# Modulation weights in steps of one k tile, and raw weight buffers in three smaller pieces

## The chip, the cores and the metric

One core of a Trainium2 chip runs the whole program in one launch. TensorE (PE) multiplies matrices, VectorE (DVE) and ScalarE (ACT) work on tiles in SBUF and PSUM, GpSimd (POOL) on tiles in SBUF, and SyncE (SP) issues every transfer from and to device memory. Each engine works through its own queue in order and waits at semaphores for the others. The metric is the device time of one execution in microseconds.

## The reference

Two layers of a transformer trunk, for 128 context tokens and 512 latent tokens (640 rows in all, width 1024):

```python
mod_ctx = (silu(c_ctx) @ w_mod[l] + b_mod[l])     # 1024 -> 6 * 1024
mod_lat = (silu(c) @ w_mod[l] + b_mod[l])
sh1, sc1, g1, sh2, sc2, g2 = split(mod, 6)
h = rmsnorm(x, norm1) * (1 + sc1) + sh1
proj = h @ w_in + b_in             # queries, keys, values, gates of three mixers
...                                # mLSTM, differential attention, neighbourhood attention
merged = gate0 * (o_da @ w_up_da) + gate1 * (o_ml @ w_up_ml) + gate2 * (o_na @ w_up_na)
x = x + g1 * (merged @ w_out)
h2 = rmsnorm(x, norm2) * (1 + sc2) + sh2
x = x + g2 * (square(relu(h2 @ w_ff1 + b_ff1)) @ w_ff2 + b_ff2)
```

The modulation is a product of two vectors (c and c_ctx) with a 1024 x 6144 matrix for each layer. It depends on no activation, so it can be worked out at any time before its values are used.

## The kernel before

**The large products.** All weights are fp32 and are split into a high part (a cast to fp32r on ACT, `whi`) and a low part (a subtraction on DVE, `wlo`), in `split`. A product is three matmuls: high by high, high by low, low by high. Weights come in blocks of 1 MB (512 KB for the `w_up` matrices) into one of two `raw` buffers of 128 x 2048 (`w_raw`, `NRAW = 2`), and the split writes them into four pairs of `whi`/`wlo` tiles (`NWT = 4`), two pairs to a block. In a-mode (weights stationary) a block is split by columns into two halves, in b-mode (weights streamed) by k tiles.

**The order of the work.** In `layer_mixers` three calls of `drive` run 12, 12 and 20 units. A unit is one block's worth of projection: it yields after each PSUM bank (4 times in a-mode, 5 in b-mode, 2 in an up unit), and after its first yield the next unit's weights are asked for. Between the yields `drive` advances the stages of the three mixers at a rate (`R_ML`, `R_DA`, `R_NA`). `layer_ff` then runs a list of 33 items through `sequence`: the product with `w_out` and the residual (`residual_pass`), the two MLP matrices in turn (`ff1`, `ff2`), and a last residual pass that also prepares the next layer.

**The modulation in the background.** The first 4 of layer 0's 12 chunks (512 columns each) are made at the start by PE. The other 8 of layer 0 and all 12 of layer 1 are made on DVE by a generator (`bg`, with `mod_chunk_dve`): for each k tile two instructions multiply 128 x 512 weights by the two vectors' scalars and add to two accumulators `macc` (of which there are two buffers in all); after 8 k tiles PE transposes the accumulators in 8 pieces, DVE sums along rows and `mod_store` adds the bias. After a layer's last chunk `mod_rows` writes the gates to device memory (`gd`), from where `layer_ff` reads them back as rows (`gload`, tiles `gr`). The weights of a chunk come as two loads of 1 MB into the same `raw` buffers that the projections use. `background()` runs the generator to its next yield. In layer 0's mixers it is called after every second unit from unit 8 to unit 40 (`BG_UNITS`), 17 times, which is just what 8 chunks of 2 steps and `mod_rows` need. In layer 0's MLP it is called at the places of `FF1_BG` and `FF2_BG`, 53 times, where 51 are needed. `layer_ff` starts with `while l not in self.gd: self.background()`.

**Who orders the queues.** The order in which the code names instructions is a priority. The framework's scheduler places each engine's instructions, and one that is ready and has its buffers may stand ahead of one named earlier. Buffers of one tag are handed out in the order in which the code asks for them.

In layer 1 there is no background work in either part, so its stages are the same program without it.

Of the kernel before, what the change touches and what calls it, by code (L numbers as in the profile page):

```python
# [11 lines left out]
F32 = mybir.dt.float32  # L12
F32R = mybir.dt.float32r
AF = mybir.ActivationFunctionType
ALU = mybir.AluOpType
AX = mybir.AxisListType
# [3 lines left out]
P = 128  # L20
D = 1024
KD = D // P
# [64 lines left out]
class Builder:  # L87
    def __init__(self, tc, I, O):
        self.tc, self.nc, self.I, self.O = tc, tc.nc, I, O
        self.uid = 0  # L90
        self.bg = None
        self.units_run = 0
        self.alt = False
        self.ff_phase = False

# [40 lines left out]
    def w_raw(self, src):  # L136

        nk, c = src.shape[1], src.shape[2]
        raw = self.T(self.wp, [P, 2048], F32, "raw", NRAW)
        r3 = raw[:, :nk * c].rearrange("p (k c) -> p k c", k=nk)  # L140
        self.nc.sync.dma_start(r3, src)
        return r3

    def w_tiles(self, n, nk):

# [3 lines left out]

        return self.w_amode_split(self.w_raw(src))  # L150

    def w_amode_split(self, r3):
        nk = r3.shape[1]
        out = []
        for j in range(2):
            h, lo = self.w_tiles(nk * P, nk)
            self.split(h, lo, r3[:, :, j * P:(j + 1) * P])
            out.append((h, lo))
        return out

    def w_bmode(self, src, extra=None):

        r3 = self.w_raw(src)
        rx = None
        if extra is not None:
            rx = self.T(self.wp, [P, 8, 16], F32, "rx", 1)
            self.nc.sync.dma_start(rx, extra)
        return self.w_bmode_split(r3, rx)

    def w_bmode_split(self, r3, rx=None):  # L170
        nk, nco = r3.shape[1] // 2, r3.shape[2]
        w = nco if rx is None else nco + 16
        out = []
        for j in range(2):
            h, lo = self.w_tiles(nk * w, nk)
            ks = slice(j * nk, (j + 1) * nk)
            self.split(h[:, :, :nco], lo[:, :, :nco], r3[:, ks, :])
            if rx is not None:
                self.split(h[:, :, nco:], lo[:, :, nco:], rx[:, ks, :])
            out += [(h[:, k, :], lo[:, k, :]) for k in range(nk)]  # L180
        return out

# [122 lines left out]
            self.modc[l][:, :, 4 * n:4 * n + 4], src,  # L305
            cv2[:, 4 * n:4 * n + 4].unsqueeze(1).to_broadcast([P, 2, 4]), op=ALU.add)

    def mod_chunk_dve(self, l, n):

        nc, I = self.nc, self.I  # L310
        acc = [self.T(self.wp, [P, 512], F32, "macc", 2) for _ in range(2)]
        for kh in range(2):
            raw = self.T(self.wp, [P, 2048], F32, "raw", NRAW)
            r3 = raw.rearrange("p (k c) -> p k c", k=4)
            nc.sync.dma_start(r3, I["w_mod"][l, n, kh])
            for k in range(4):
                kk = kh * 4 + k
                for v in range(2):
                    s = self.cc3[:, v, kk:kk + 1]
                    if kk == 0:  # L320
                        nc.vector.tensor_scalar_mul(acc[v], r3[:, k, :], s)
                    else:
                        nc.vector.scalar_tensor_tensor(acc[v], r3[:, k, :], s, acc[v], op0=ALU.mult, op1=ALU.add)  # L323
                if kk in ((1, 3, 5) if l else (3,)):
                    yield
        red = self.st(8)
        for v in range(2):
            tp = self.t_ps()
            for j in range(4):
                nc.tensor.transpose(tp[:, j * P:(j + 1) * P], acc[v][:, j * P:(j + 1) * P], self.ident)  # L330
            nc.vector.tensor_reduce(red[:, 4 * v:4 * v + 4], tp.rearrange("p (j c) -> p j c", j=4), axis=AX.X, op=ALU.add)
        self.mod_store(l, n, red.rearrange("p (v j) -> p v j", v=2))
        yield

    def mod_norm_cols(self, l, which):

# [145 lines left out]
        return g  # L482

    def w_up(self, src):
        r3 = self.w_raw(src)
        h, lo = self.w_tiles(1024, 4)
        self.split(h, lo, r3)
        return [(h[:, :, q * P:(q + 1) * P], lo[:, :, q * P:(q + 1) * P]) for q in range(2)]
# [25 lines left out]
    def drive(self, units, stages, rate, w, tail):  # L514

        units = list(units)
        credit = 0.0
        waiting = None  # L520
        sdone = False

        def step_stage():
            nonlocal waiting, sdone
            while True:
                if sdone:
                    return
# [12 lines left out]
                return  # L540

        def pick():
            for i, u in enumerate(units):
                if u[2] is None or u[2] in self.labels:
                    return units.pop(i)
            return units.pop(0) if units else (tail, None, None)

        cur = units.pop(0)
        while cur[1] is not None:
            while cur[2] is not None and cur[2] not in self.labels:  # L550
                step_stage()
            nxt = pick()
            wn = None
            first = True
            for _ in cur[1](w):
                if first:
                    wn = nxt[0]()
                first = False
                credit += rate
                while credit >= 1.0:  # L560
                    credit -= 1.0
                    step_stage()
            self.units_run += 1
            if self.units_run in BG_UNITS:
                self.background()
            cur, w = nxt, wn
        while not sdone:
            step_stage()
        return w
# [888 lines left out]
    def layer_ff(self, l, merged, w, last):  # L1458
        tc, nc, I, O = self.tc, self.nc, self.I, self.O
        with tc.tile_pool(name=f"xp{l}", bufs=1, reuse_waits="tile") as xp:  # L1460
# [33 lines left out]
            def ff1_first():  # L1494
                def prep():
                    return self.w_amode(I["w_ff1"][l, 0]), self.w_raw(I["w_ff1"][l, 1])

                def run(wr):
                    w = wr[0] + self.w_amode_split(wr[1])
                    us[0] = [(self.act_slice(), self.act_slice()) for _ in range(4)]  # L1500
                    for a, b in BANKS:
                        for j in range(4):
                            o = self.gemm_a(w[j], h2, a, b)
                            self.ff1_evac(l, j, *us[0][j], o, a, b)
                            if a == 0 and todo:
                                todo.pop(0)()
                            yield a > 0 and j >= 1
                    self.background()
                return prep, run

            def ff1(ch, i):
                def run(w):
                    if i == 0:
                        us[ch] = [(self.act_slice(), self.act_slice()) for _ in range(4)]
                    for q in range(2):
                        j = ch * 4 + i + q
                        for a, b in BANKS:
                            o = self.gemm_a(w[q], h2, a, b)
                            self.ff1_evac(l, j, *us[ch][i + q], o, a, b)
                            if (q, a) in FF1_BG:  # L1520
                                self.background()
                            yield True
                    if i == 0 and 1 <= ch <= TT:
                        t = ch - 1
                        nc.gpsimd.tensor_tensor(xs[t], xs[t], gr[4 if t < 4 else 5], op=ALU.add)
                return (lambda: self.w_amode(I["w_ff1"][l, (ch * 4 + i) // 2])), run

            def ff2(ch, cp):
                def run(w2):
                    sl = slice(cp * 512, (cp + 1) * 512)  # L1530
                    for t in range(TT):
# [1 line left out]
                        tmp = self.T(xp, [P, 512], F32, "tmp", 2)  # L1533
                        nc.vector.tensor_tensor(tmp, o, gr[2 if t < 4 else 3][:, sl], op=ALU.mult)  # L1534
                        nc.gpsimd.tensor_tensor(xs[t][:, sl], xs[t][:, sl], tmp, op=ALU.add)  # L1535
                        if t in FF2_BG:
                            self.background()
                        yield True
                return (lambda: self.w_bmode(I["w_ff2"][l, ch, cp])), run

# [125 lines left out]
    def run(self):  # L1666
        tc, nc, I = self.tc, self.nc, self.I
        with ExitStack() as ctx:
# [4 lines left out]
            def bg():  # L1673
                for l in range(DEPTH):
                    if l:
# [3 lines left out]
                        yield  # L1679
                        yield  # L1680
                        fin()
                    for n in range(4 if l == 0 else 0, 12):
                        yield from self.mod_chunk_dve(l, n)
                    self.mod_rows(l)
                    yield
            self.bg = bg()
# [3 lines left out]


NMM, NS2, NTP = 2, 2, 2
NRAW, NWT = 2, 4
FIN_AT, PREP_AT, FIRST = 4, 3, 7
R_ML, R_DA, R_NA = 1.1, 1.6, 1.6
ML_FIRST = 2
CARRY = 3
LAG1, LAG2 = 1, 1
FF1_BG, FF2_BG = ((0, 0), (1, 256)), (1, 3)
BG_UNITS = range(8, 42, 2)  # L1700
NSL, NOT, NV = 16, 12, 9

OUT_SHAPES = {
# [12 lines left out]
def lay_out(x):  # L1716
# [9 lines left out]
    def halves(w):  # L1726
# [16 lines left out]
        "w_up_na": blocks(x["w_up_na"], 256),  # L1743
        "w_out": halves(x["w_out"]),
        "w_ff2": halves(x["w_ff2"]),
        "w_mod": x["w_mod"].reshape(L, 2, 4, P, 12, 512).transpose(0, 4, 1, 3, 2, 5),
        "w_mod0": x["w_mod"][0, :, :2048].reshape(KD, P, 2048),
        "xT": xs.T.reshape(KD, P, NT).transpose(1, 0, 2),
        "x_sample": x["x_sample"],
# [37 lines left out]
```

## Time and profile before

| | |
|---|---|
| median of 3 runs | 2491.02 us (2487.69 to 2491.09) |
| the profiled execution, its own time | 2490.52 us |
| its span, first to last instruction | 2488.7 us |
| PE busy | 2415.0 us, 97% of the span |
| DVE busy | 1523.0 us, 61% |
| ACT busy | 905.1 us, 36% |
| mean granted TensorE clock | 0.993 of full speed |
| transferred | 286.52 MB, 115 GB/s over the span |

The profile is one execution, 1.8 us longer outside its span than inside it. PE's busy time counts overlapping matmuls once; a gap in it is time in which PE waited.

### The profile page before, as it was taken

Reading aid. Unit: us, or ns where it says so; the run is one execution under the profiler, and the core shown is the slowest. Engines: PE = TensorE matmul, PEld = TensorE weight load, DVE = VectorE, ACT = ScalarE, POOL = GpSimd, SP = SyncE. Lnnn points to the kernel's source line nnn. Section 1 sums busy time; section 2 is a strip of 40 time slices with the busy share of each in tenths; the row PEclk is TensorE's granted clock in tenths of the full one; section 3 lists DMA queues with packets and bytes.
Section 4 is the critical chain, followed back from the end, with each engine's and each line's share of the span. In section 5 each row is a group of like instructions: output and inputs, shape, how many; then the busy total and the mean of one; then the engine's idle time right before and its main releaser. Section 6 shows DMA issues by size and latency. Waiting matters only on the chain. (4 is left out here: it accounts for less than half of the span.)

```text
span 2488.7 us, 39544 instructions
## 1 busy us (share of the span) xinstructions
PE 2415.0 (97%) x15776; PEld 2266.3 (91%) x15776; DVE 1523.0 (61%) x2804; ACT 905.1 (36%) x1954; POOL 640.9 (26%) x701
## 2 busy tenths in 40 slices
PE   6999999999999999999999999999999999999998
PEld 4999999999998898999989999999989889999997
DVE  5557788566634899998565547674443464444444
ACT  4332354334433422223353334443443353322232
POOL 0122122233412233332021212222352312233301
PEclk8999999999999999999999999999999999999999
DMA  7323323333353334444332222223232722222221
GB/s 271 105 94 117 112 97 135 121 117 123 139 190 130 119 136 152 153 136 153 103 122 97 96 90 87 76 82 111 74 116 86 261 85 85 68 85 68 85 68 60
DMA packets 73706, 286.52 MB, mean 115 GB/s; under 512 B 9889, under 2 KB 21249, under 8 KB 49969
## 3 DMA queue, kind: packets, MB, share of 16 engines
q1 hardware_dynamic: 73520, 283.99, 33.3%
q8 instruction: 124, 2.03, 0.3%
q14 instruction: 62, 0.50, 0.1%
HBM read 257.60 MB, written 26.35 MB: 114 GB/s over the span
## 5 line engine op out<-in xcount | busy, mean ns | idle before, releaser
L191 PE MATMUL mm<-act,whi 128*128 128x384 f32 (+1 forms) x2176 | 699.4, 321 | 11.7 <-DVE act L503 3.4
L192 PE MATMUL mm<-act,whi 128*128 128x384 f32 (+1 forms) x2176 | 687.5, 316 | 0.0
L193 PE MATMUL mm<-act,wlo 128*128 128x384 f32 (+1 forms) x2176 | 686.0, 315 | 0.0
L217 ACT CAST whi<-raw 128x1024 fp32r<-128x1024 f32 x296 | 310.9, 1050 | 921.3 <-PE mm L192 439.3
L218 DVE TENSOR_TENSOR wlo<-raw,whi 128x1024 fp32r<-128x1024 f32 x296 | 383.8, 1297 | 381.3 <-ACT whi L217 327.2
L191 PEld LDWEIGHTS mm<-act,whi 128*128 128x128 f32 x2176 | 413.9, 190 | 17.5 <-issue 6.0
L192 PEld LDWEIGHTS mm<-act,whi 128*128 128x128 f32 x2176 | 414.3, 190 | 0.0
L193 PEld LDWEIGHTS mm<-act,wlo 128*128 128x128 f32 x2176 | 413.8, 190 | 0.0
L1535 POOL TENSOR_TENSOR x<-x,tmp 128x512 f32<-128x512 f32 x120 | 194.0, 1623 | 448.5 <-DVE tmp L1534 448.5
L210 PE MATMUL mm<-whi,act 128*128 128x256 f32 (+2 forms) x800 | 270.0, 338 | 0.0
L212 PE MATMUL mm<-whi,act 128*128 128x256 f32 (+2 forms) x800 | 267.1, 334 | 0.0
L211 PE MATMUL mm<-wlo,act 128*128 128x256 f32 (+2 forms) x800 | 266.4, 333 | 0.0
L323 DVE SCALAR_TENSOR_TENSOR macc<-raw,cc,macc 128x512 f32<-128x512 f32 x280 | 232.2, 874 | 20.0 <-DMA raw<-w_mod 19.6
L212 PEld LDWEIGHTS mm<-whi,act 128*128 128x128 f32 x800 | 152.0, 190 | 14.3
L211 PEld LDWEIGHTS mm<-wlo,act 128*128 128x128 f32 x800 | 152.1, 190 | 14.0
L210 PEld LDWEIGHTS mm<-whi,act 128*128 128x128 f32 x800 | 152.1, 190 | 14.0
L210 PE MATMUL t<-whi,act 128*128 128x512 f32 (+1 forms) x416 | 158.5, 381 | 1.7 <-ACT act L217 1.5
L211 PE MATMUL t<-wlo,act 128*128 128x512 f32 (+1 forms) x416 | 157.8, 379 | 0.0
L212 PE MATMUL t<-whi,act 128*128 128x512 f32 (+1 forms) x416 | 157.8, 379 | 0.0
L192 PE MATMUL t<-act,whi 128*128 128x256 f32 (+1 forms) x512 | 146.4, 286 | 0.0
L193 PE MATMUL t<-act,wlo 128*128 128x256 f32 (+1 forms) x512 | 146.4, 286 | 0.0
L191 PE MATMUL t<-act,whi 128*128 128x256 f32 (+1 forms) x512 | 146.2, 286 | 0.0
(286 smaller groups left out, 4168.6 us busy)
## 6 DMA issues: line engine op xcount, KB each, us to landing
raw<-w_in SPq DMA_DIRECT2D x64, 1024.0 KB
raw<-w_ff SPq DMA_DIRECT2D x64, 1024.0 KB
raw<-w_mod SPq DMA_DIRECT2D x48, 1024.0 KB
mgd<-act SPq DMA_DIRECT2D x32, 320.0 KB
act<-mgd SPq DMA_DIRECT2D x32, 320.0 KB
raw<-w_out SPq DMA_DIRECT2D x8, 1024.0 KB
gr<-gd SPq DMA_DIRECT2D x12, 512.0 KB
act<-rd SPq DMA_DIRECT2D x16, 320.0 KB
```

The costliest lines, as they stand in the source:

```text
L191: nc.tensor.matmul(o, wh, ah, start=(k == 0), stop=False)
L192: nc.tensor.matmul(o, wh, al, start=False, stop=False)
L193: nc.tensor.matmul(o, wl, ah, start=False, stop=(k == nk - 1))
L210: nc.tensor.matmul(o, ah, wh, start=(first and k == 0), stop=False)
L211: nc.tensor.matmul(o, ah, wlo, start=False, stop=False)
L212: nc.tensor.matmul(o, al, wh, start=False, stop=(last and k == nk - 1))
L217: self.nc.scalar.copy(hi, src)
L218: self.nc.vector.tensor_tensor(lo, src, hi.bitcast(F32), op=ALU.subtract)
L323: nc.vector.scalar_tensor_tensor(acc[v], r3[:, k, :], s, acc[v], op0=ALU.mult, op1=ALU.add)
L1535: nc.gpsimd.tensor_tensor(xs[t][:, sl], xs[t][:, sl], tmp, op=ALU.add)
```

## The change

The generator's step becomes one k tile. Each step first asks for the next k tile's weights (256 KB, 128 x 512) into one of two tiles of their own (`mraw`), then multiplies the tile that was asked for a step earlier. The host lays `w_mod` out by k tile. In layer 0's mixers the steps are taken at a rate of 0.55 for each yield of a unit, from unit 8 on; in its MLP after every bank of `ff1` but the first four, and after every tile of `ff2`. Layer 1's chunks are transposed into one PSUM tile of two banks (`s_ps`) and summed by one instruction. The raw weights come as two loads of 128 x 1024 into three such buffers (`NRAW = 3`), and an a-mode block is split in four pieces of 128 x 512 and not in two of 128 x 1024.

```diff
     def w_raw(self, src):
         nk, c = src.shape[1], src.shape[2]
-        raw = self.T(self.wp, [P, 2048], F32, "raw", NRAW)
-        r3 = raw[:, :nk * c].rearrange("p (k c) -> p k c", k=nk)
-        self.nc.sync.dma_start(r3, src)
-        return r3
+        n = 1024 // c
+        out = []
+        for k in range(0, nk, n):
+            r3 = self.T(self.wp, [P, 1024], F32, "raw", NRAW).rearrange("p (k c) -> p k c", k=n)
+            self.nc.sync.dma_start(r3, src[:, k:k + n])
+            out.append(r3)
+        return out
...
-    def w_amode_split(self, r3):
-        nk = r3.shape[1]
+    def w_amode_split(self, raws):
+        n = raws[0].shape[1]
+        nk = n * len(raws)
         out = []
         for j in range(2):
             h, lo = self.w_tiles(nk * P, nk)
-            self.split(h, lo, r3[:, :, j * P:(j + 1) * P])
+            for i, r3 in enumerate(raws):
+                self.split(h[:, i * n:(i + 1) * n], lo[:, i * n:(i + 1) * n], r3[:, :, j * P:(j + 1) * P])
...
-    def mod_chunk_dve(self, l, n):
+    def mod_chunks(self, l, ns):
...
+        items = [(n, k) for n in ns for k in range(KD)]
+
+        def load(i):
+            raw = self.T(self.wp, [P, 512], F32, "mraw", 2)
+            nc.sync.dma_start(raw, I["w_mod"][l, items[i][0], items[i][1]])
+            return raw
+        nxt = load(0)
         yield
+        for i, (n, k) in enumerate(items):
+            raw, nxt = nxt, load(i + 1) if i + 1 < len(items) else None
+            if k == 0:
+                acc = [self.T(self.wp, [P, 512], F32, "macc", 2) for _ in range(2)]
+            for v in range(2):
+                s = self.cc3[:, v, k:k + 1]
+                if k == 0:
+                    nc.vector.tensor_scalar_mul(acc[v], raw, s)
+                else:
+                    nc.vector.scalar_tensor_tensor(acc[v], raw, s, acc[v], op0=ALU.mult, op1=ALU.add)
+            yield
+            if k < KD - 1:
+                continue
+            red = self.st(8)
+            both = self.s_ps() if l else None
+            for v in range(2):
+                tp = both[:, v * 512:(v + 1) * 512] if l else self.t_ps()
+                for j in range(4):
+                    nc.tensor.transpose(tp[:, j * P:(j + 1) * P], acc[v][:, j * P:(j + 1) * P], self.ident)
+                if not l:
+                    nc.vector.tensor_reduce(red[:, 4 * v:4 * v + 4], tp.rearrange("p (j c) -> p j c", j=4), axis=AX.X, op=ALU.add)
+            if l:
+                nc.vector.tensor_reduce(red, both.rearrange("p (j c) -> p j c", j=8), axis=AX.X, op=ALU.add)
+            self.mod_store(l, n, red.rearrange("p (v j) -> p v j", v=2))
+            yield
...
                 while credit >= 1.0:
                     credit -= 1.0
                     step_stage()
+                if self.units_run >= BG_FROM:
+                    self.bg_credit += R_BG
+                    while self.bg_credit >= 1.0:
+                        self.bg_credit -= 1.0
+                        self.background()
             self.units_run += 1
-            if self.units_run in BG_UNITS:
-                self.background()
...
-                            if (q, a) in FF1_BG:
-                                self.background()
+                            self.background()
...
-                        if t in FF2_BG:
-                            self.background()
+                        self.background()
...
-NRAW, NWT = 2, 4
+NRAW, NWT = 3, 4
...
-FF1_BG, FF2_BG = ((0, 0), (1, 256)), (1, 3)
-BG_UNITS = range(8, 42, 2)
+BG_FROM, R_BG = 8, 0.55
```

## Rows read from the trace of the kernel before

**Rows 1.** Windows: mixers 0, MLP 0, mixers 1, MLP 1; busy us (count), clock, DMA.

```profile
39.63:757.56 717.93, 693.65 (x5033) 673.75 (x5034) 471.19 (x954) 277.95 (x647) 188.63 (x249) 0.99 0.38 127
757.56:1278.61 521.05, 518.45 (x2899) 466.76 (x2898) 411.33 (x625) 169.04 (x324) 139.17 (x85) 1.00 0.37 128
1278.61:1976.33 697.72, 682.82 (x4984) 665.15 (x4983) 381.14 (x812) 279.06 (x662) 186.17 (x261) 1.00 0.32 108
1976.33:2488.70 512.37, 502.94 (x2777) 454.27 (x2776) 240.80 (x378) 167.85 (x304) 122.57 (x86) 1.00 0.22 78
```

**Rows 2.** The same windows, instructions on the accumulators alone: PE, PE loads, DVE.

```profile
39.63:757.56 717.93, 9.19 (x64) 7.22 (x64) 93.40 (x128) 0.99 0.38 127
757.56:1278.61 521.05, 13.96 (x96) 10.85 (x96) 156.77 (x192) 1.00 0.37 128
```

**Rows 3.** Waits of PE, 40 to 760 us: total us, times, longest us.

```profile
PE t L812 <- DVE C L821: 5.7, 4, 3.5
PE mm L191 <- ACT act L1173: 3.2, 1, 3.2
...
PE mm L191 <- DVE act L501: 1.7, 1, 1.7
```

**Rows 4.** Timeline of DVE in mixers 0: start, us, instruction, what idle time waited for.

```profile
152.36 0.88 DVE L321 TENSOR_SCALAR macc<-raw,cc 128x512 f32<-128x512 f32 x2 [2.51 <-DMA raw<-w_mod]
153.16 4.65 DVE L323 SCALAR_TENSOR_TENSOR macc<-raw,cc,macc 128x512 f32<-128x512 f32 x3
...
472.64 6.29 DVE L323 SCALAR_TENSOR_TENSOR macc<-raw,cc,macc 128x512 f32<-128x512 f32 x7
```

**Rows 5.** Timeline of PE just behind those two places.

```profile
158.12 0.80 PE L812 MATMUL t<-v,act 128*128 128x129 f32 x2 [3.46 <-DVE C L821]
...
479.70 0.44 PE L191 MATMUL mm<-act,whi 128*128 128x384 f32 x1 [3.18 <-ACT act L1173]
```

**Rows 6.** Windows of 4 us behind the two gaps; the clock is third from the end.

```profile
158.00:162.00 4.00, 3.88 (x18) 3.88 (x19) 4.00 (x10) 0.86 (x3) 2.20 (x3) 0.50 0.00 0
162.00:166.00 4.00, 4.00 (x26) 4.00 (x26) 2.36 (x9) 0.17 (x1) 0.00 (x0) 0.81 0.50 147
480.00:484.00 4.00, 4.00 (x17) 4.00 (x16) 2.56 (x6) 1.87 (x4) 3.72 (x9) 0.62 0.41 109
484.00:488.00 4.00, 4.00 (x30) 4.00 (x29) 1.35 (x3) 1.37 (x2) 0.00 (x0) 0.95 0.22 87
```

**Rows 7.** Timelines of SP and DVE: one 1 MB load, and who waited for it.

```profile
946.25 0.33 SPq L315 DMA_DIRECT2D raw<-w_mod  x1
...
950.95 0.75 DVE L323 SCALAR_TENSOR_TENSOR macc<-raw,cc,macc 128x512 f32<-128x512 f32 x1 [1.76 <-DMA raw<-w_mod]
```

**Rows 8.** Timeline of SP: loads for layer 1, the gates' write, their first read.

```profile
41.39 0.90 SPq L1678 DMA_DIRECT2D colv<-cols  x2
...
727.77 0.39 SPq L363 DMA_DIRECT2D gd<-stg  x1
...
743.39 1.13 SPq L1471 DMA_DIRECT2D gr<-gd  x1
```

**Rows 9.** Groups by line and form on ACT and DVE: busy, mean ns, idle before.

```profile
L217 ACT CAST whi<-raw 128x1024 fp32r<-128x1024 f32 x296 | 310.9, 1050 | 921.3 <-PE mm L192 439.3 <-PE t L212 140.9 <-PE mm L212 129.9
...
L1448 ACT ACTIVATE act<-relu 128x384 fp32r<-128x384 f32 x64 | 33.6, 524 | 1.8
...
L218 DVE TENSOR_TENSOR wlo<-raw,whi 128x1024 fp32r<-128x1024 f32 x296 | 383.8, 1297 | 381.3 <-ACT whi L217 327.2 <-PE s L1268 52.2
...
L1450 DVE TENSOR_TENSOR act<-relu,act 128x384 fp32r<-128x384 f32 x64 | 35.6, 556 | 1.8
```

**Rows 10.** Timelines of PE and DVE where mixers 0 end and MLP 0 begins.

```profile
757.56 0.39 PE L210 MATMUL t<-whi,act 128*128 128x512 f32 x1
...
761.64 0.56 DVE L218 TENSOR_TENSOR act<-act,act 128x384 fp32r<-128x384 f32 x1 [1.46 <-ACT act L217]
...
774.12 0.69 DVE L1401 TENSOR_TENSOR tmp<-t,gr 128x512 f32<-128x512 f32 x1 [0.41 <-PE t L212]
```

More of the change, by code (lines that the diff above doesn't have):

```diff
@@ L92, in __init__ @@
         self.units_run = 0
+        self.bg_credit = 0.0
         self.alt = False
@@ L161, in w_bmode @@
     def w_bmode(self, src, extra=None):
-        r3 = self.w_raw(src)
+        raws = self.w_raw(src)
         rx = None
@@ L167, in w_bmode, with w_bmode_split @@
             self.nc.sync.dma_start(rx, extra)
-        return self.w_bmode_split(r3, rx)
-    def w_bmode_split(self, r3, rx=None):
-        nk, nco = r3.shape[1] // 2, r3.shape[2]
+        return self.w_bmode_split(raws, rx)
+    def w_bmode_split(self, raws, rx=None):
+        nk, nco = raws[0].shape[1:]
         w = nco if rx is None else nco + 16
         out = []
-        for j in range(2):
+        for j, r3 in enumerate(raws):
             h, lo = self.w_tiles(nk * w, nk)
-            ks = slice(j * nk, (j + 1) * nk)
-            self.split(h[:, :, :nco], lo[:, :, :nco], r3[:, ks, :])
+            self.split(h[:, :, :nco], lo[:, :, :nco], r3)
             if rx is not None:
-                self.split(h[:, :, nco:], lo[:, :, nco:], rx[:, ks, :])
+                self.split(h[:, :, nco:], lo[:, :, nco:], rx[:, j * nk:(j + 1) * nk, :])
             out += [(h[:, k, :], lo[:, k, :]) for k in range(nk)]
@@ L306, in mod_store @@
             cv2[:, 4 * n:4 * n + 4].unsqueeze(1).to_broadcast([P, 2, 4]), op=ALU.add)
-    def mod_chunk_dve(self, l, n):
+    def mod_chunks(self, l, ns):
         nc, I = self.nc, self.I
[L311 to L332, printed above, removed]
-        yield
@@ L484, in w_up @@
     def w_up(self, src):
-        r3 = self.w_raw(src)
+        r3, = self.w_raw(src)
         h, lo = self.w_tiles(1024, 4)
@@ L1506, in run @@
                                 todo.pop(0)()
+                            if a > 0:
+                                self.background()
                             yield a > 0 and j >= 1
-                    self.background()
                 return prep, run
@@ L1535, in run @@
                         nc.gpsimd.tensor_tensor(xs[t][:, sl], xs[t][:, sl], tmp, op=ALU.add)
-                        if t in FF2_BG:
-                            self.background()
+                        self.background()
                         yield True
@@ L1681, in bg @@
                         fin()
-                    for n in range(4 if l == 0 else 0, 12):
-                        yield from self.mod_chunk_dve(l, n)
+                    yield from self.mod_chunks(l, range(4 if l == 0 else 0, 12))
                     self.mod_rows(l)
@@ L1745, in lay_out @@
         "w_ff2": halves(x["w_ff2"]),
-        "w_mod": x["w_mod"].reshape(L, 2, 4, P, 12, 512).transpose(0, 4, 1, 3, 2, 5),
+        "w_mod": x["w_mod"].reshape(L, KD, P, 12, 512).transpose(0, 3, 1, 2, 4),
         "w_mod0": x["w_mod"][0, :, :2048].reshape(KD, P, 2048),
```

## The prediction

> **What bounds the kernel now.** I read the stages first, then PE's waits in the one stage that has any to spare, then what the engine that was waited for did just before. The windows by stage show PE busy in 518.45 of 521.05 us of layer 0's MLP, so nothing can be gained there, though DVE is busiest there (411.33 us). Layer 0's mixers leave PE idle for 717.93 - 693.65 = 24.3 us, layer 1's, the same program without background work, for 697.72 - 682.82 = 14.9 us [rows 1]. The first take 20.2 us longer. 9.2 us of that is PE's own part of the background, the 64 transposes [rows 2], which the change keeps. So some 11 us at most is what background work costs layer 0's mixers beyond its transposes, and no other stage has a prize.
>
> Where it is lost can be read. PE's waits for DVE name the mLSTM state (L821), an evacuation chain through ACT (L1173) and an up unit's evacuation (L501) [rows 3]. Before the first, DVE had stood 2.51 us waiting for a modulation load and then run five accumulations, 5.4 us in all; before the second it ran seven in a row, 6.29 us [rows 4]. PE then stood 3.46 and 3.18 us [rows 5]. After each gap the granted clock is near half, 1.2 instead of 2.4 GHz: 0.50 and 0.81, and 0.62 and 0.95 over two windows of 4 us, so 4 x (0.50 + 0.19) = 2.8 us and 4 x (0.38 + 0.05) = 1.7 us more are lost [rows 6]. The two blocks thus cost 3.46 + 2.8 + 3.18 + 1.7 = 11.1 us, and the single wait at L501 1.7 us [rows 3], whose part I can't separate. That is 11 to 13 us from the waits and 11 us from the comparison of the two layers.
>
> **The change part by part.**
>
> *Steps of one k tile.* A step's DVE work falls from eight accumulations in a row (four in layer 1's steps) to two, some 1.5 us. With two small buffers at most four can stand ready together, 3 us. Blocks of 6.29 and 7.9 us left 3.18 and 3.46 us of PE idle [rows 4, 5], so 3 to 4.4 us of a block were covered by what PE still had to do; a block of 3 us leaves nothing. Upper bound of the gain: 12.8 us. Lower bound: nothing, if the blocks return in another place. I take 9.5 us, the 11.1 us of the two blocks less a seventh for what a wait of 1 or 2 us elsewhere gives back.
>
> *Loads of their own, one step ahead.* A 1 MB load landed 950.95 - 946.25 = 4.7 us after its issue, and DVE stood 1.76 us for it [rows 7]. A load of a quarter lands in between a quarter of that, 1.2 us, and all of it, 4.7 us; I take 3 us. With two in flight and 1.5 us of work to each, a k tile comes every (3 + 1.5) / 2 = 2.2 us, a chunk's eight in 18 us. DVE may stand up to a microsecond at a load, but then runs only 1.5 us, and the sum, 2.5 us, is still under the cover worked out above. In layer 0's mixers this costs nothing.
>
> *When the steps really run.* The rate of 0.55 sets a priority and not a time. The loads of layer 1's columns, which the generator first names in layer 0's MLP, that is after 757.56 us, were issued at 41.39 us [rows 8]. The modulation loads were held back so far only because they queued for the projections' buffers. With their own tiles they are held by the accumulators alone: a chunk's eight k tiles may start when the chunk before it has been transposed, and will run as fast as loads and DVE allow, then rest. So DVE gets about 20 us of dense work per chunk, not an even spread. In layer 0's MLP, DVE has 521.05 - 411.33 = 110 us free and PE never waits; the accumulations are the same 192 in number [rows 2], so I charge 0 there, with a bound under the rivals.
>
> *The end of layer 0's mixers.* Unit 8 to unit 43 yield 18 + 42 + 64 = 124 times, so 0.55 x 124 = 68 steps are taken. Eight chunks need 1 + 8 x 9 steps and `mod_rows` one, 74. Six steps are left to the loop at the head of `layer_ff`: half of the last chunk, its transposes, and the write of `gd`. Before, that write went out at 727.77 us, 30 us ahead of the first product with `w_out` at 757.56 [rows 8, 10]. If all runs in the order named, DVE is free of the last up unit at 762.2 [rows 10], then works 10 accumulations (7.5 us, of which loads draw out 3 us more) and some 3 us of sums and small operations, and PE starts at about 775: a stall of 17.5 us, and 2.8 us of slow clock behind it. If the scheduler lets the accumulations go early, as it did with the loads above, they start after the seventh chunk's transposes, named behind the first of eight up tiles; 26 us are left for a chunk of 18 us, and PE stands nothing. The reads of the gates are covered in both cases as long as `gd` is out some 5 us before their first use at 774.12 [rows 10]. Between 0 and 20 us I take 3.5: rows 8 speak for the early order, but this is the stretch in which the merge tiles, `w_out` and the residual rows are loaded and small loads will queue.
>
> *Three raw buffers of half a block.* The look-ahead falls from two blocks to one and a half. Cover: the casts wait for PE to free the weight tiles (439.3, 140.9 and 129.9 us), and no load is among their first releasers [rows 9]. With 33 items in 521.05 us an item takes 16 us [rows 1], so half a block less still leaves a lead of several times the 4.7 us of a 1 MB load. Price 0; if that cover were gone, each block would be late by up to 4.7 us. On SP the 136 blocks of 1 MB become two issues each and the 40 modulation loads 160, 256 issues more at 0.33 us [rows 7], 84 us of a queue that has 2488 and mostly waits for buffers. A modulation load that waits there for DVE holds up the loads behind it, as it does now; the lead of the weights covers that.
>
> *Splits in four.* From 1050 ns at 1024 columns and 524 at 384, a cast of 512 is about 629 ns by a straight line, so two cost 0.21 us more than one; a subtraction (1297 and 556) about 704, so 0.11 us more [rows 9]. There are 42 a-mode blocks in a layer and two extra pairs in each: in a mixer stage (26 blocks) ACT gets 11 us and DVE 6 us more of 698 to 718, in an MLP 7 and 4 us. ACT is busy 280 of 700 us and DVE at most 79% [rows 1], and PE does not wait for a split now. I charge 0.5 us for the four stages; none at the low end, 3 us at the high.
>
> *Layer 1's sums in one instruction, PSUM of `s_ps`.* Fewer DVE instructions where PE doesn't wait: 0.
>
> **Sum.** -9.5 + 3.5 + 0.5 = -5.5 us against the profiled execution's 2490.5, so 2485.0 us. The median of the runs shown, 2491.02, is 0.5 us above that execution, within its runs' spread. About 0.2%, 5 us, is what a measurement of this kernel can tell from no change.
>
> **The rivals.**
>
> *The blocks come back (0.30).* Since the chunks are not spread by the rate, DVE is dense for 20 us after each chunk's transposes, and delays of 1 to 3 us fall on other chains, among them the gaps after which the clock halves. Rows 8 speak for it; against it, a block is now at most 3 us. About half of the 9.5 us is gained, and the boundary takes it: 2488 to 2491. No change.
>
> *The forced steps at the head of the MLP (0.12, the other side).* The order as named: 17.5 + 2.8 us of stall against the 9.5 us gained, 2490.5 + 20.3 - 9.5 + 0.5 = 2502 us. It decides from the point at which PE's first product with `w_out` comes over 14 us late.
>
> *Small loads starve DVE (0.08).* If each of layer 0's 96 MLP loads makes DVE stand as the 1 MB load did, 1.76 us, that is 169 us where 110 are free [rows 7, 1], and PE loses the rest, 59 us at most. If half of them do, 85 us, it stays hidden. With two thirds, 113 us, and the splits' 4 us, some 7 us come through and more where DVE is dense, 15 us: 2490.5 - 9.5 + 4 + 15 = 2500 us. The Trainium skill's page "DMA: Bandwidth & Descriptors", section Bandwidth, speaks for this one: it asks for 1 MiB or more in a transfer to come near the peak rate, and the change goes from 1 MB to 256 KB; the trace has no load of these weights in the smaller size to set beside it.
>
> **Chances and range.** My forecast has 0.50, with its own range of 2477 (the whole 12.8 us, nothing lost) to 2486.5. Faster by over 0.2% (under 2486): 0.46 of that, 0.02 of the first rival: 0.48. Slower (over 2496): 0.12 + 0.06 and 0.02 of the first rival: 0.20. The same: 0.32. The range of 2477 to 2501 leaves out the worst of the last two rivals and little below.
>
> **What would show it.** Right: no gap of over 3 us in layer 0's mixers from 110 to 720 us, no granted clock near 0.5 there, DVE runs of at most four accumulations, and the mixers some 9 us shorter. A chunk's accumulations bunched behind the transposes of the one before would show the order that I expect. At the boundary, the first product with `w_out` should follow the last up tile within 4 us. Wrong: a gap ahead of that product with the eighth chunk's transposes or the gates' sum as the releaser; PE waits in layer 0's MLP; ACT casts that wait for a load; or a stage without background work, layer 1's mixers, that changes by more than the 2 us I allow the splits.

## The result and the profile after

The changed kernel takes 2507.7 us (median of 4 runs, 2504.5 to 2508.7), the kernel before 2489.98: a ratio of 1.0075, 95% interval 1.0063 to 1.0087. It is slower by 0.75%, where 2485 us and a range to 2501 were forecast. The profiled execution has a span of 2506.9 us.

The windows by stage of the changed kernel; each mixer stage ends with its last up tile, and the columns are those of [rows 1]:

```profile
39.28:759.54 720.26, 695.24 (x5029) 676.15 (x5030) 475.00 (x999) 282.14 (x699) 184.59 (x249) 0.99 0.39 122
759.54:1289.56 530.02, 520.09 (x2903) 467.88 (x2902) 413.95 (x653) 172.63 (x356) 122.84 (x85) 1.00 0.42 132
1289.56:1992.34 702.78, 684.40 (x4985) 667.41 (x4984) 384.31 (x864) 283.78 (x714) 185.42 (x261) 0.99 0.32 103
1992.34:2506.93 514.59, 503.99 (x2777) 455.62 (x2775) 254.42 (x410) 170.25 (x336) 117.62 (x86) 0.99 0.25 83
```

Cut in the same way, the kernel before has 718.1, 520.9, 697.9 and 512.2 us. So +2.2 in layer 0's mixers, +9.1 in its MLP, and +4.9 and +2.4 in layer 1, which has no background work at all. In the MLP, PE is busy 1.6 us longer than in [rows 1] and idle 9.9 us instead of 2.6; DVE's busy time there has hardly moved (414.0 us, 411.3 before).

Layer 0's mixers did gain where it was forecast, and lost it again elsewhere. PE's timeline and the windows of 4 us at the two places of [rows 5, 6]:

```profile
159.98 0.49 PE L823 MATMUL t<-v,act 128*128 128x129 f32 x2 [2.03 <-DVE C L839]
...
472.67 0.36 PE L196 MATMUL mm<-act,whi 128*128 128x256 f32 x1 [1.86 <-DVE act L1189]
```

```profile
158.00:162.00 4.00, 2.02 (x12) 1.94 (x13) 3.21 (x10) 2.48 (x9) 1.83 (x3) 0.87 0.29 90
162.00:166.00 4.00, 4.00 (x19) 4.00 (x18) 1.24 (x5) 0.00 (x0) 0.00 (x0) 0.70 0.10 41
470.00:474.00 4.00, 2.14 (x16) 1.85 (x15) 1.96 (x4) 1.45 (x3) 3.09 (x5) 1.00 0.43 58
474.00:478.00 4.00, 4.00 (x31) 4.00 (x31) 2.22 (x7) 2.67 (x5) 2.47 (x7) 1.00 0.55 207
```

The gaps are 2.03 and 1.86 us instead of 3.46 and 3.18, and the clock loses 4 x (0.13 + 0.30) = 1.7 us and nothing, instead of 2.8 and 1.7. When PE's instructions are paired with their like in the trace of before, the changed kernel gains 2.1 us at the first place and 3.9 at the second, and is 7.1 us ahead at 570 us. Of the first gain 1.0 us is gone by 230 us: one update of the mLSTM state (L839) stands at 199 us behind a maximum that waits for ScalarE (L845), which it did not before, and PE's gap is 2.84 us instead of 0.64 (run 10 tests the like of it in layer 1). Timelines of DVE and PE:

```profile
199.05 0.16 DVE L845 TENSOR_TENSOR st<-st,act 128x1 f32<-128x1 f32 x1 [3.62 <-ACT st L842]
199.12 0.34 DVE L839 SCALAR_TENSOR_TENSOR C<-C,decb,t 128x129 f32<-128x129 f32 x1
...
199.52 0.49 PE L830 MATMUL t<-v,act 128*128 128x129 f32 x2 [2.84 <-DVE C L839]
```

At 610 us it is 2.1 ahead: two waits for GpSimd copies in the neighbourhood attention (3.3 us, the third row below) came in between, and behind them the granted clock is 0.63 and 0.52 over two windows of 4 us from 590 us on, 4 x (0.37 + 0.48) = 3.4 us more. At 720 it is 3.4 ahead, at 770 it is 3.5 behind. PE's waits, 40 to 760 us, then 720 to 770, then 760 to 1290:

```profile
PE mm L196 <- DVE act L518: 5.2, 8, 0.8
PE t L830 <- DVE C L839: 4.1, 3, 2.8
PE s L1288 <- POOL act L943: 3.3, 2, 2.3
...
PE mm L196 <- DVE act L518: 5.0, 7, 0.8
PE t L342 <- DVE macc L333: 1.0, 1, 1.0
...
PE s L342 <- DVE macc L333: 6.6, 9, 1.5
PE s L405 <- POOL xn L399: 2.1, 2, 1.2
```

So 6 us of waits lie in the up units at the end of the mixers, and in the MLP it is the transposes of the accumulators (L342) that wait for the last accumulation (L333). The loads are late. The first two rows are DVE's waits for modulation loads from 760 to 1290 us, in the kernel before and in the changed one. Below them stands the longest such wait of the whole trace, which lies in the mixers, with the issue that it waited for (timelines of SP and DVE).

```profile
DVE macc L323 <- DMA raw<-w_mod: 13.5, 10, 2.1
...
DVE macc L333 <- DMA mraw<-w_mod: 26.7, 27, 2.6
```

```profile
597.78 0.62 SPq L1221 DMA_DIRECT2D vb<-rpb  x1
598.50 0.88 SPq L320 DMA_DIRECT2D mraw<-w_mod  x2
...
602.88 0.75 DVE L333 SCALAR_TENSOR_TENSOR macc<-mraw,cc,macc 128x512 f32<-128x512 f32 x1 [5.63 <-DMA mraw<-w_mod]
```

### The profile page after: what moved, and what is told of

It is laid out like the page before. It is cut to its first block, busy times and chain, and to the rows that moved or that the text cites. A ratio compares the mean times of both kernels' runs of the same rounds, so it can differ in the third digit from the quotient of the medians.

```text
span 2506.9 us, 40575 instructions
## 1 busy us (share of the span) xinstructions
PE 2420.7 (97%) x15776; PEld 2273.1 (91%) x15776; DVE 1546.2 (62%) x2960; ACT 921.0 (37%) x2122; POOL 614.9 (25%) x701
## 3 DMA queue, kind: packets, MB, share of 16 engines
q8 instruction: 124, 2.03, 0.3%
## 5 line engine op out<-in xcount | busy, mean ns | idle before, releaser
L222 ACT CAST whi<-raw 128x512 fp32r<-128x512 f32 (+1 forms) x464 | 331.4, 737 | 942.2 <-PE mm L197 500.9
L223 DVE TENSOR_TENSOR wlo<-raw,whi 128x512 fp32r<-128x512 f32 (+1 forms) x464 | 432.1, 948 | 396.7 <-ACT whi L222 382.3
L196 PEld LDWEIGHTS mm<-act,whi 128*128 128x128 f32 x2176 | 414.0, 190 | 14.0 <-ACT whi L222 4.0
L1553 POOL TENSOR_TENSOR x<-x,tmp 128x512 f32<-128x512 f32 x120 | 173.4, 1448 | 481.9 <-DVE tmp L1552 481.9
L333 DVE SCALAR_TENSOR_TENSOR macc<-mraw,cc,macc 128x512 f32<-128x512 f32 x280 | 229.7, 845 | 41.3 <-DMA mraw<-w_mod 41.0
## 6 DMA issues: line engine op xcount, KB each, us to landing
raw<-w_in SPq DMA_DIRECT2D x128, 512.0 KB
raw<-w_ff SPq DMA_DIRECT2D x128, 512.0 KB
raw<-w_out SPq DMA_DIRECT2D x16, 512.0 KB
gr<-gd SPq DMA_DIRECT2D x12, 512.0 KB
```

Source lines behind the costliest of these rows:

```text
L196: nc.tensor.matmul(o, wh, ah, start=(k == 0), stop=False)
L222: self.nc.scalar.copy(hi, src)
L223: self.nc.vector.tensor_tensor(lo, src, hi.bitcast(F32), op=ALU.subtract)
L333: nc.vector.scalar_tensor_tensor(acc[v], raw, s, acc[v], op0=ALU.mult, op1=ALU.add)
```

## The experiments

Each run was timed next to the kernel before on the same chip, in 4 to 11 executions. Stage times are those of one profiled execution, cut as above. One execution of a stage can stand some 4 us from another whose instructions are in the same order (the tenth run below), so smaller differences are read only where a trace shows their place. "Ledger theory" in the expectations means the list of losses by stage above.

| run | ratio, 95% interval | us | mixers 0 | MLP 0 | mixers 1 | MLP 1 |
|---|---|---|---|---|---|---|
| before | 1 | 2490.0 | 718.1 | 520.9 | 697.9 | 512.2 |
| changed | 1.0075 (1.0063 to 1.0087) | 2507.7 | 720.3 | 530.0 | 702.8 | 514.6 |
| 1 steps alone | 1.0068 (1.0053 to 1.0083) | 2504.9 | 723.5 | 537.3 | 699.5 | 512.0 |
| 2 raw pieces alone | 1.0074 (1.0062 to 1.0086) | 2507.9 | 723.4 | 528.1 | 701.8 | 513.7 |
| 3 splits in four alone | 1.0034 (1.0021 to 1.0047) | 2498.5 | 719.3 | 529.3 | 695.2 | 512.6 |
| 4 four raw pieces | 1.0017 (1.0008 to 1.0026) | 2493.6 | 713.4 | 525.9 | 700.6 | 512.6 |
| 5 rate 0.65 | 1.0152 (1.0139 to 1.0165) | 2527.1 | 722.1 | 547.5 | 700.8 | 513.7 |
| 6 second accumulators | 1.0070 (1.0055 to 1.0085) | 2507.0 | 717.2 | 529.0 | 707.6 | 513.7 |
| 7 half the accumulations | 1.0034 (1.0020 to 1.0047) | 2499.8 | 722.9 | 522.4 | 699.6 | 513.7 |
| 8 loads three steps ahead | 1.0040 (1.0025 to 1.0055) | 2498.6 | 718.4 | 519.6 | 702.4 | 513.6 |
| 9 the same, rate 0.60 | 1.0090 (1.0075 to 1.0106) | 2510.3 | 733.4 | 520.8 | 700.7 | 513.7 |
| 10 one instruction moved | 1.0072 (1.0059 to 1.0084) | 2507.7 | 724.0 | 531.3 | 697.7 | 515.6 |
| 11 own loads, early | 0.9984 (0.9975 to 0.9993) | 2485.5 | 719.4 | 517.5 | 695.4 | 511.9 |
| 12 the parts that paid | 0.9978 (0.9969 to 0.9987) | 2483.9 | 710.0 | 519.3 | 696.9 | 512.6 |

**1 and 2: each half alone.** Run 1 takes the steps at the changed kernel's places, with the whole raw buffers, their loads and splits as before; run 2 takes the raw pieces and leaves the background in its old portions.

```diff
-                if kk in ((1, 3, 5) if l else (3,)):
-                    yield
+                yield
```

> The steps alone: one k tile to a step, at the places and the rate of the changed kernel, but with the weights in 1 MB loads from the two large raw buffers as before, the splits in two and layer 1's chunks summed in two pieces. Ledger theory (the loss has four places: about 6 us at the end of layer 0's mixers from the forced steps, 7 us in layer 0's MLP where transposes wait for accumulations that have only just run, 5 us in layer 1's mixers and 2 to 3 us in layer 1's MLP from the raw pieces): this kernel keeps the forced steps and drops the rest, so layer 1's stages are back at 697.7 and 512.4 us, and the time is 2491 to 2498 us. Rival (the new calls are the whole cause): about 2507 us with layer 1's stages as before. Rival (own tiles and pieces are the whole cause): 2484 to 2490 us.

> The raw pieces alone: three buffers of 128 x 1024, loads of 512 KB, splits in four; the background as before (its 1 MB halves now come as two pieces of two k tiles from the same buffers). Ledger theory: layer 1's mixers near 702.6 and its MLP near 514.7 us as in the changed kernel, layer 0 may lose as much again in its mixers; 2496 to 2504 us. Rival (layer 1's longer stages only come from where the queues happen to fall in the changed kernel): 2488 to 2493 us, with layer 1's stages as before.

Run 1 came out near the rival's number, run 2 above both: each half costs what the whole does, and they don't add. Run 1 loses most in layer 0's MLP (16 us, in an execution 8.6 us slower than the median), run 2 in all four stages, so in layer 1 too, where there is no background work.

Late loads don't explain run 1: DVE waits for them 4.1 us in that stage. Its sums stay in the two PSUM tiles `t` that `ff2` uses too, and PE's transposes wait for an evacuation on DVE that frees such a tile (PE's longest entry there):

```profile
PE t L330 <- DVE tmp L1537: 8.0, 7, 1.9
```

The changed kernel has its sums in `s_ps` and no such wait. So that part, charged 0 in the prediction, seems to matter once steps are fine; no run changes the tile alone.

**3 and 4: what the raw pieces cost.** Run 3 has two whole buffers and only splits their blocks in four; run 4 is run 2 with four half blocks.

```diff
-            self.split(h, lo, r3[:, :, j * P:(j + 1) * P])
+            for i in (0, nk // 2):
+                ks = slice(i, i + nk // 2)
+                self.split(h[:, ks], lo[:, ks], r3[:, ks, j * P:(j + 1) * P])
```

> The kernel before with one edit: the stages whose raw blocks were split in two instructions are split in four, while the big raw buffers and the background pieces stay as they were. If the extra instructions on VectorE and GpSimd are what makes layer 1 longer with the small raw buffers (layer 1's stages went from 697.9 to 701.8 us and from 512.2 to 513.7), then layer 1's mixers take 701 to 703 us, its MLP 513 to 514, and the whole 2496 to 2508 us. If it is the shorter look-ahead of three half blocks against two whole ones, the stages stay at 697 to 699 and 512 to 513 us, and the whole at 2488 to 2493.

> The run with the small raw buffers alone (2507.9 us), with four half-block buffers in place of three, so that as many bytes stand ahead as in the kernel before. If the look-ahead is what cost, the stages come back to those of before (mixers 718 to 720, MLP 521 to 523, then 698 to 700 and 512 to 513 us) and the whole to 2488 to 2494. If it is the pieces and their instructions, it stays at 2500 to 2508.

Three buffers against four are 14 us (2507.9 and 2493.6), as the look-ahead theory had it, though layer 1's mixers stay long in run 4 and its MLP 0 takes 5 us more than before. The casts' waits for raw loads, 40 to 1280 us, in run 2, and then in run 4:

```profile
ACT whi L221 <- DMA raw<-w_ff: 86.6, 18, 10.1
ACT whi L221 <- DMA raw<-w_in: 10.7, 5, 4.7
```

```profile
ACT whi L221 <- DMA raw<-w_ff: 11.3, 4, 5.2
```

So half a block less of look-ahead was not free. The waits alone don't give the price: in the kernel before, the casts wait 56.8 us for raw loads, 51.3 of them in layer 0's MLP, where PE is idle for 2.6 us in all. But the changed kernel has three buffers too, and its casts wait 10.2 us for raw loads: with the modulation's loads out of these buffers three are enough. Run 2's price is not a term of the changed kernel, which is why the halves don't add. Run 3's 9 us lie in layer 0's MLP, not in layer 1 as expected. PE's gaps there are mostly at the same PSUM tiles `t` as in run 1: 4.4 us for a sum that DVE has not yet done (L333) and 1.6 us for an evacuation (L1536).

**5: no forced steps.** The changed kernel at a rate of 0.65.

> The changed kernel with a rate of 0.65 in place of 0.55: 80 steps fall in layer 0's mixers, the 74 of layer 0 are done before the last up units and none is forced. Ledger theory: PE's first product with w_out no longer stands behind the last chunk, 6 us less, 2501 to 2503 us. Rival (the stretch loses its 6 us to the merge tiles' and w_out's loads or to PE's changed order there): 2506 to 2509 us.

Both numbers missed. Between 720 and 770 us only some 2.5 us are lost instead of 7, but the MLP takes 547.5 us. Here the way of a late load can be followed: timelines of DVE and PE, then windows of 4 us.

```profile
1097.70 1.42 DVE L333 SCALAR_TENSOR_TENSOR macc<-mraw,cc,macc 128x512 f32<-128x512 f32 x2 [2.02 <-DMA mraw<-w_mod]
1099.03 1.22 DVE L223 TENSOR_TENSOR wlo<-raw,whi 128x1024 fp32r<-128x1024 f32 x1
1100.17 0.55 DVE L1467 TENSOR_TENSOR relu<-relu 128x384 f32<-128x384 f32 x1
1100.76 0.56 DVE L1468 TENSOR_TENSOR act<-relu,act 128x384 fp32r<-128x384 f32 x1
...
1102.16 0.80 PE L217 MATMUL t<-whi,act 128*128 128x512 f32 x1 [2.88 <-DVE act L1468]
```

```profile
1100.00:1104.00 4.00, 1.84 (x4) 1.49 (x5) 3.90 (x8) 0.00 (x0) 0.00 (x0) 0.70 0.61 184
1104.00:1108.00 4.00, 4.00 (x21) 3.33 (x20) 2.06 (x5) 0.00 (x0) 1.67 (x2) 0.87 0.46 143
```

DVE stands 2.02 us at an accumulation whose weights are not there; the evacuation that PE needs next (L1468) is queued behind it, PE stands 2.88 us, and the clock falls to 0.70 and 0.87, 4 x (0.30 + 0.13) = 1.7 us more. The same gap stands at 975.93, 1040.31 and 1163.68 us with 2.5 to 2.7 us, behind last stands of 2.48, 1.70 and 0.69 us. It doesn't grow with the stand, so what else is queued there, two accumulations and a split, has a part in it; this was not taken apart.

**6, 7 and 8: late loads, or too much work on DVE?** Run 6 gives every other chunk of layer 1 accumulators of its own; run 7 leaves accumulations out; run 8 loads layer 1's k tiles three steps ahead.

```diff
-        nxt = load(0)
+        ahead = 3 if l else 1
+        nxt = [load(i) for i in range(ahead)]
...
-            raw, nxt = nxt, load(i + 1) if i + 1 < len(items) else None
+            raw = nxt.pop(0)
+            if i + ahead < len(items):
+                nxt.append(load(i + ahead))
```

> The changed kernel with a second pair of accumulators for every other chunk of layer 1 (in a tile that layer 0's MLP leaves unused), so that a chunk's accumulations need not wait for the transposes of the one before. Ledger theory (PE waits in layer 0's MLP because a chunk's chain of loads and accumulations, 25 us, fills the time between two transposes): the waits of the transposes, 6.6 us, go, and the time is 2499 to 2502 us. Rival (DVE has no room: dense from evacuations, splits and accumulations together): they stay, 2506 to 2510 us.

> The changed kernel, but the second of each k tile's two vectors accumulates only its first k tile in layer 1: 84 of its 192 accumulations are left out (so the modulation of layer 1 lacks these products), while loads, transposes and calls stay. If the density of VectorE's accumulations made layer 0's MLP longer, TensorE's waits for evacuations at the steps go away, the stage takes 521 to 524 us and the whole 2497 to 2501. If it is the loads that come late, VectorE still stands at them, the stage takes 526 to 530 and the whole 2503 to 2508.

> The changed kernel with the weights of layer 1's modulation loaded three steps ahead instead of one, in four tiles (two of them lie in memory that is idle in layer 0's MLP). If accumulations that stand at the head of VectorE's queue for a load are what made layer 0's MLP longer (VectorE waited 41 us for those loads in 39 waits), that stage falls from 530.0 to 522 to 524 us and the whole to 2499 to 2502. If the density of the accumulations is the cause, the waits for loads go away, TensorE still waits for evacuations, the stage stays at 528 to 531 and the whole at 2505 to 2509.

PE's waits in layer 0's MLP: the first row of run 6; those of run 7 over 0.2 us, and DVE's wait for its loads; those of run 8 over 0.2 us.

```profile
PE t L217 <- DVE act L1472: 4.6, 3, 2.0
```

```profile
PE s L407 <- POOL xn L401: 3.2, 1, 3.2
PE t L344 <- DVE macc L335: 1.0, 1, 1.0
PE mm L196 <- DVE act L520: 0.6, 1, 0.6
DVE macc L335 <- DMA mraw<-w_mod: 54.8, 37, 3.3
```

```profile
PE s L411 <- POOL xn L405: 3.2, 4, 1.5
```

Run 6 came out at its rival's time, run 7 as the density theory, run 8 as the loads' theory, whose forecast for the stage was some 2 us longer. DVE never stood for a load in run 8's MLP, and 54.8 us in run 7's. With more accumulators the transposes no longer wait, but evacuations do: the accumulations only stand elsewhere in DVE's queue. With all accumulations and early loads the stage takes 519.6 us, less than before; with late loads and half the accumulations 522.4. Each cure is enough, so neither cause is one by itself: work and stands together must fit between two sets of transposes, and in the changed kernel they don't. What the change added to DVE's time there is mostly stands (26.7 us in place of 13.5), for the 192 accumulations were there before.

**9: both cures.** Run 8 with a rate of 0.60, at which all 74 steps fit into the mixers.

> The run with layer 1's loads three steps ahead (2498.6 us), with the rate of the steps in the mixers at 0.60 in place of 0.55, so that layer 0's 74 steps all fit into its mixers and none is left for the head of the MLP. If the forced steps and the late last chunk cost at the boundary, the 7 us that TensorE lost between 720 and 770 us fall to 0 to 3, the MLP stays at 519 to 523 us, and the whole is 2492 to 2496. If the rate itself is what made the run at 0.65 long (2527.1 us, MLP 547.5 us with late loads), the MLP is at 527 us or more and the whole above 2502.

Two of three parts held: PE's waits between 720 and 776 us fall to those of the kernel before (2.5 us in two, for the up tiles alone), 1.2 us are lost across the boundary, and the MLP takes 520.8 us. But the mixers took 15 us more than in run 8, in one place at least by the same cause. Timelines of SP, DVE and PE:

```profile
546.97 10.33 SPq L1227 DMA_DIRECT2D vb<-rpb  x2
557.35 0.92 SPq L323 DMA_DIRECT2D mraw<-w_mod  x2
...
562.56 0.75 DVE L339 SCALAR_TENSOR_TENSOR macc<-mraw,cc,macc 128x512 f32<-128x512 f32 x1 [5.21 <-DMA mraw<-w_mod]
...
565.80 0.28 DVE L1324 COPY act<-s 128x128 f32<-128x128 f32 x1
...
566.14 1.42 PE L1337 MATMUL t<-act,v 128*64 128x128 f32 x10 [3.46 <-DVE act L1324]
```

SP's two issues of `vb` span 10.33 us, since the second goes out only at their end; the modulation load stands behind it, DVE stands 5.21 us for the load, and PE 3.46 us for the copies that follow on DVE. The other places of these 15 us were not followed. The same wait of 5.63 us in the changed kernel (602.88, above) cost PE under a microsecond: what is queued behind it decides.

**10: layer 1, without background work.** The framework's scheduler had set one update of the mLSTM state (L839) behind a maximum that waits for ScalarE (L845). One ordering edge puts it back; every other instruction keeps its place.

```diff
+                if (l, h, i) == (1, 2, 2):
+                    for later in (mx, my):
+                        self.tc.add_manual_dep(later.ins, first.ins.name, ORDER, reason="order")
```

> The changed kernel with one instruction of VectorE set one place forward, 1449 us into the run: the update of the mLSTM state C of layer 1's third head (L839) stands ahead of the two maxima (L845, L846), as in the kernel before, and not between them; every other instruction of every engine keeps its place. If that place is what made layer 1's mixers longer, TensorE's gap of 3.03 us there falls to 1.5 us or less, the mixers go from 702.8 to 698.5 to 700.5 us and the whole to 2503 to 2505. If the wait for ScalarE ahead of it is only a sign of engines that run late there, the gap stays near 3 us, the mixers at 702 to 703 and the whole at 2506 to 2509.

Timelines of DVE and PE in the changed kernel, then of DVE in run 10:

```profile
1449.33 0.16 DVE L845 TENSOR_TENSOR st<-st,act 128x1 f32<-128x1 f32 x1 [3.81 <-ACT st L842]
1449.41 0.35 DVE L839 SCALAR_TENSOR_TENSOR C<-C,decb,t 128x129 f32<-128x129 f32 x1
...
1449.81 0.49 PE L830 MATMUL t<-v,act 128*128 128x129 f32 x2 [3.03 <-DVE C L839]
```

```profile
1448.73 0.35 DVE L840 SCALAR_TENSOR_TENSOR C<-C,decb,t 128x129 f32<-128x129 f32 x1 [0.69 <-PE t L831]
1451.51 0.16 DVE L848 TENSOR_TENSOR st<-st,act 128x1 f32<-128x1 f32 x1 [2.43 <-ACT st L845]
```

PE's gap is gone and the stage is as long as before the change, 697.7 us. Not all of these 5.1 us belong to the moved instruction. Paired instruction by instruction, the two executions part by 3.7 us there; 2.4 us come earlier, at 1410 us, at a gap of 2.29 us in the changed kernel whose order run 10 leaves alone, and 1 us is lost again later. The whole did not show it: 2507.7 us again, and this execution lost 3.7 us in layer 0's mixers whose order is untouched. So the place and its price of about 4 us are read from the traces, and the median, whose interval is some 3 us to either side, neither shows nor excludes them.

**11 and 12: early loads on the kernel before.** Run 11 is the kernel before with layer 1's modulation alone in steps; its weights come two k tiles at a time into two tiles that are idle in this stage.

```diff
+            raw = self.T(self.xp, [P, D], F32, ("pad", "nf")[i % 2], 1).rearrange("p (k c) -> p k c", k=2)
+            nc.sync.dma_start(raw, I["w_mod"][l, n, j // 2][:, 2 * (j % 2):2 * (j % 2) + 2])
```

> The kernel before with one part alone: layer 1's modulation in steps of one k tile at the changed kernel's places, its weights two k tiles at a time into two tiles of its own that are idle in layer 0's MLP. Layer 0's modulation, the two whole raw buffers and the splits in two stay, and the instructions of the mixers keep their order. If steps cost nothing once no accumulation stands at a load, layer 0's MLP takes 519 to 522 us (520.9 before), the other stages are as before and the whole is 2486 to 2491. If accumulations in single steps delay evacuations by themselves, the MLP takes 526 to 532 and the whole 2495 to 2501.

> The pieces that paid, put together: four half-block raw buffers, layer 0's modulation in the pieces of the kernel before, layer 1's modulation in steps of one k tile whose weights come two k tiles at a time into two tiles of their own that are idle in layer 0's MLP, and the update of C in the place of the kernel before. By the stages of the runs that had each piece (start 39.4, mixers 713.4, MLP 520, mixers 697, MLP 512.6) 2482 us, so 2480 to 2486. If each edit sets other instructions in other places, and with that new waits in stages that it does not touch, the stages don't add: 2488 to 2496.

Run 11's MLP takes 517.5 us, 3.4 less than before, and is the cleanest test: the same steps at the same places, with DVE waiting 0.7 us in all for their loads. The whole, 0.16% under the kernel before, is a little under its forecast too. In the profiled execution 2.5 us of the gain lie in layer 1's mixers, whose order is that of before, so the size of the gain stays open; but steps cost nothing here. Run 12 adds run 4's raw pieces and run 10's edge and is the fastest, 0.22% under the kernel before; against run 11 the intervals overlap.

## Why the prediction was wrong, step by step

- *Steps of one k tile*: right in kind and place, too large in size. Of the 9.5 us that were taken, 6.0 came at the two places, and 1.0 of them went again behind the first. The lead of 7.1 us at 570 us has other small gains in it.
- *Loads of their own, one step ahead*: **this step failed first.** A load did land after some 4 us (598.50 to 602.88), within the bounds, where 3 were taken. But the sum took each load as issued on time and DVE's stand as at most a microsecond. In the MLP DVE stood up to 2.6 us at a load and 26.7 us in all. Where SP's queue was held up, by up to 10 us in run 9, stands of 5.6 us (changed kernel) and 5.2 (run 9) followed. The cover worked out from PE's two gaps was also used for every place; the transposes, which wait for the last accumulation itself, have none.
- *When the steps really run*: the order was right (each chunk's accumulations bunch behind the transposes of the one before), the conclusion was not. A free 110 us on DVE is a mean over the stage; a chunk has 27 to 30 us between its transposes (run 11), and its accumulations, from the second chunk on, took 18 to 24 us before and 22 to 28 with the stands. Charged 0, measured 9.1 us. Runs 7, 8, 9 and 11 each take it away, run 7 all but 1.5 us.
- *The end of layer 0's mixers*: the place was right, and the product with `w_out` did follow the last up tile at once, but the size was not right. 3.5 us were taken, about 6 were lost (from 3.4 ahead to 3.5 behind, of which 1.2 stay without forced steps in run 9), not as a stall ahead of the MLP but in seven waits of up to 0.8 us in the up units. `gd` went out at 765.86 us and delayed nothing.
- *Three raw buffers*: free in the changed kernel, for a reason that was not given. The cover was misread: a row that names a group's first three releasers can't show that no load is among the rest, and the casts did wait 56.8 us for loads. With the modulation still in them the price would have been 14 us (runs 2 and 4).
- *Splits in four*: the casts cost what was worked out, the subtractions more, as the groups by form of the changed kernel show beside [rows 9]:

```profile
L222 ACT CAST whi<-raw 128x512 fp32r<-128x512 f32 x336 | 197.0, 618 | 574.6 <-PE mm L197 236.9 <-PE mm L217 175.5 <-PE t L217 135.5
L223 DVE TENSOR_TENSOR wlo<-raw,whi 128x512 fp32r<-128x512 f32 x336 | 268.7, 823 | 160.3 <-ACT whi L222 159.3
```

  A cast took 618 ns (629 worked out), a subtraction 823 (704), so two subtractions cost 0.35 us more than one, not 0.11. What was left out is the order: layer 1, charged under 0.5 us, lost 7.3. One moved instruction holds about 4 of them in the mixers (run 10). Runs 2 and 4 have that gap (3.06 and 2.67 us), run 3 has not, so in these runs it comes with the pieces of half a block and not with the number of splits. In the MLP one GpSimd instruction holds 2 us by the trace (below).
- *The rivals*: the blocks did come back, as stands at loads, and took more than was gained. *Small loads starve DVE* was nearest in time (2500 us) and right that loads are the cause, but its threshold was not: DVE stood 26.7 us in the MLP, far under the 110 us that are free. The Trainium skill's page "DMA: Bandwidth & Descriptors", section Bandwidth, asks for transfers of 1 MiB. Size was not what decided here: for loads of 256 KB three steps ahead (run 8) DVE did not wait at all in this stage.

Open are the cause of the waits for GpSimd copies between 570 and 610 us in layer 0's mixers; whether the PSUM tiles `t` are all of what run 3's extra splits cost (8.4 us in a stage with DVE time to spare); and how much of the loss at the boundary belongs to the forced steps alone.

## What to carry to other kernels

Free time of an engine in a stage says nothing about an in-order queue: ask of each instruction that waits for a load what is queued behind it, and load so far ahead that the slowest entry of the issuing queue fits in between. A part that is cut finer needs its loads as early as before, counted in time and not in steps. Compare the instruction order of untouched stages too, since a scheduler that sees other durations may move an instruction there, and one moved instruction cost about 4 us.

## What was not expected of the hardware

A GpSimd operation on 128 x 1 elements (L387), 0.56 us in the median here, took 3.13 us in layer 1's MLP, and PE stood 3.20 us behind it; the longest such wait in that stage of the kernel before is 1.2 us. Timelines of GpSimd, DVE and PE:

```profile
2053.82 3.13 POOL L387 TENSOR_TENSOR st<-st,mhalf 128x1 f32<-128x1 f32 x1 [10.60 <-ACT xn L392]
...
2053.66 1.28 DVE L223 TENSOR_TENSOR wlo<-raw,whi 128x512 fp32r<-128x512 f32 x2
2054.86 0.49 DVE L418 TENSOR_TENSOR act<-hf,act 128x128 fp32r<-128x128 f32 x2
2055.26 1.29 DVE L223 TENSOR_TENSOR wlo<-raw,whi 128x512 fp32r<-128x512 f32 x2
...
2058.23 1.50 PE L405 MATMUL s<-ident,xn 128*128 128x128 f32 x8 [3.20 <-POOL xn L399]
```

It lasts about as long as DVE's unbroken run of operations with two inputs from SBUF, from 2053.66 to 2056.55. The Trainium skill's page "SBUF — State Buffer", section "SBUF: two separate sides", says that such operations of VectorE and a GpSimd operation exclude each other; the rows agree with it, but no run here takes the one away to test the other.
